# Turned weight products: wide, narrow, narrow, wide in place of wide, narrow, wide, narrow

## The chip, the cores and the metric

The kernel runs on one core of one Trainium2 chip. The metric is the device time of one execution in microseconds (us), as the median of several executions.

## The reference

One decoder block for 256 tokens of 2048 features: a half-step feed-forward, retention and sliding-window heads from one projection, an output projection, cross-attention into 256 memory tokens, a second half-step feed-forward and a last norm. Nearly all of the work is products with weights:

```python
def swiglu(x, w_gate, w_up, w_down):
    return (jax.nn.silu(x @ w_gate) * (x @ w_up)) @ w_down
...
h = h + 0.5 * swiglu(rms_norm(h, ffn1_norm[l]), ffn1_w_gate[l], ffn1_w_up[l], ffn1_w_down[l])
n = rms_norm(h, mix_norm[l])
rq, rk, rv, rg, sq, sk, sv = jnp.split(n @ w_in[l], IN_SPLITS, axis=-1)
...
h = h + jnp.concatenate([ret, swa.astype(h.dtype)], axis=-1) @ w_out[l]
h = h + memory_cross_attention(rms_norm(h, xa_norm[l]), rms_norm(mem, mem_norm[l]), xa_wq[l], xa_wkv[l], xa_wo[l])
h = h + 0.5 * swiglu(rms_norm(h, ffn2_norm[l]), ffn2_w_gate[l], ffn2_w_up[l], ffn2_w_down[l])
return rms_norm(h, final_norm)
```

All of it is float32, with D_MODEL 2048 and D_FF 5632.

## The kernel before

Every float32 factor is used as the exact sum of a high and a low half, `wh` and `wl` for a weight, the two halves of `blk` for an input. ScalarE makes the high half by a copy (`halves`, line 68), VectorE the low half by a subtraction (line 73). A product is high times high plus high times low plus low times high.

The weights come in pieces of 128 x 1024 (tile `wf`, two pieces per DMA, issued by SyncE). One piece is one step of a stream that `run_stream` writes out in program order: at step `at`, `prepare` brings the splitting of pieces up to `at + 3` (LOOKAHEAD), so that `wh` and `wl`, four buffers each, are made some steps ahead. Small tasks (norms, attention) are put between the steps. A group of steps that fill the same accumulator `acc` is a `Unit`; the accumulators have two buffers.

There are two kinds of products. `by_tokens` holds the tokens in the array and calls `three` (lines 361 to 363): three matmuls of 512 columns each. `by_weights`, the turned product that the change touches, holds the weights. A step of it has four tiles `k` of 128 rows and two halves `f` of 128 output features, and for each `(k, f)` it runs two matmuls on the accumulator half `acc[:, f]`:

- a wide one (line 214): the high half of the weights against both halves of the input, 512 columns
- a narrow one (line 215): the low half of the weights against the high half of the input, 256 columns, which is added to the first 256 columns

In the last tile of a unit, the narrow one stands ahead of the wide one (lines 211 and 212). Each matmul has weights of its own, which TensorE loads (LDWEIGHTS, 128 columns) while the matmul ahead of it runs. There are 600 such steps, 4800 wide and 4800 narrow matmuls. A unit over the 2048 features of the model has four steps, 32 wide and 32 narrow ones.

TensorE works its instructions off in the order in which they are written, so the order of the two loops in `by_weights` is the order on the engine.

Of the kernel before, what the change touches and what calls it, by code (L numbers as in the profile page):

```python
# [17 lines left out]
P = 128  # L18
S = 256
# [18 lines left out]
def decoder_block(ctx: ExitStack, tc: tile.TileContext, a: dict, out: bass.AP):  # L38
    nc = tc.nc
# [14 lines left out]
    def blk(dt=F32R):  # L54
        """Four tiles of 128 features by 256 tokens, each as its high and its low half."""
        return work.tile([P, 4, 2, S], dt, tag="blk", name=nm("blk"), bufs=13)
# [13 lines left out]
    def halves(hi, lo, src):  # L70
        """src as the exact sum of two short halves."""
        copy(hi, src)
        nc.vector.tensor_tensor(lo, src, hi, ALU.subtract)  # L73
# [18 lines left out]

    # ------------------------------------------------------------------
    # The stream of weight products, with small tasks between its steps.
    # A product either holds the tokens in the array and gives [tokens, 512 columns], or (turned)
    # holds the weights in it and gives [256 columns, tokens], as two parts still to be added.
    st = {}
    units = []
    tasks = []
# [5 lines left out]
    def when(ready, delay, fn):  # L105
        """fn after a delay, and once ready() holds."""
        def attempt():
            if ready():
                fn()
            else:  # L110
                later(1, attempt)
        later(delay, attempt)
# [16 lines left out]
    class Unit:  # L129
        """One group of n output columns of a product with w, laid out in pieces of 1024 per partition."""  # L130

# [5 lines left out]
        def steps(self):  # L137
            """(unit, block, its tiles of 128 rows, piece of w, first, last)"""
            per = 1024 // self.n
            out = [  # L140
                (self, b, range(i * per, (i + 1) * per), b * (4 // per) + i)
                for b in self.blocks
                for i in range(4 // per)
            ]
            return [x + (i == 0, i == len(out) - 1) for i, x in enumerate(out)]
# [13 lines left out]
    def pin():  # L159
        """Keeps each engine's instructions so far in the order in which they were written."""  # L160
        prev = {}
        for ins in nc.cur_bb.bb.instructions:
            if ins.engine in prev:
                tc.add_manual_dep(
                    ins, prev[ins.engine].name,
                    mybir.DependencyInfo(mybir.DependencyClass.NoSync, mybir.DependencyReason.DATA),
                    reason="program order",
                )
            prev[ins.engine] = ins

    def run_stream():
# [11 lines left out]
        ready = {}  # L183
# [20 lines left out]

        def by_weights(acc, x, wh, wl, first, last):
            for k in range(4):
                for f in range(2):
                    fs = slice(f * P, (f + 1) * P)
                    both, main = acc[:, f, :], acc[:, f, :S]
                    if last and k == 3:  # L210
                        nc.tensor.matmul(main, wl[:, k, fs], x[:, k, 0, :], start=False, stop=False)  # L211
                        nc.tensor.matmul(both, wh[:, k, fs], x[:, k, :, :], start=False, stop=True)  # L212
                    else:
                        nc.tensor.matmul(both, wh[:, k, fs], x[:, k, :, :], start=first and k == 0, stop=False)  # L214
                        nc.tensor.matmul(main, wl[:, k, fs], x[:, k, 0, :], start=False, stop=False)  # L215

# [37 lines left out]

    # ------------------------------------------------------------------
    def turn(src):
        """Transposes src(t, kk) [128 tokens, 128] into two banks of [128, 2, 256]."""
        tp = [tmp_ps() for _ in range(2)]
        for kk in range(4):
            for t in range(2):  # L260
                nc.tensor.transpose(
                    tp[kk // 2][:, (kk % 2) * S + t * P : (kk % 2) * S + (t + 1) * P], src(t, kk), ident
                )
        return tp

    def split_turned(tp, gcol):
        """The exact halves of a turned block, each feature times its gain where there is one."""
        x = blk()
        for b in range(2):
            v = tp[b].rearrange("p (k s) -> p k s", k=2)  # L270
            if gcol is None:
                ks = slice(2 * b, 2 * b + 2)
                halves(x[:, ks, 0, :], x[:, ks, 1, :], v)
            else:
                gained(x[:, 2 * b : 2 * b + 2], v, gcol + 2 * b)
        return x

    def gained(x, v, gcol):
        """x = the exact halves of v, each feature times its gain."""
        for k in range(v.shape[1]):  # L280
            g = gains[:, gcol + k : gcol + k + 1]
            copy(x[:, k, 0, :], v[:, k, :], scale=g)
            nc.vector.scalar_tensor_tensor(x[:, k, 1, :], v[:, k, :], g, x[:, k, 0, :], ALU.mult, ALU.subtract)  # L283

    class Norm:
        """Blocks of a normed and split input [features, tokens], made as the blocks of its source come.

        The blocks lack 1 / rms: the results are multiplied by it, per token."""

# [7 lines left out]
        def block(self, b, src):  # L297
            """src: the block's tiles, [128, n, 256] each."""
            x = blk()
# [6 lines left out]
        def stat(self, src):  # L306
            """Adds the squares of a block to the sums."""
            for v in src:
# [11 lines left out]
        def finish(self):  # L320
            """1 / rms of the tokens, on the partitions."""
            tp = tmp_ps()
# [11 lines left out]
        def spread(self):  # L334
            """The same along the free axis, on every partition."""
            tp = tmp_ps()
# [15 lines left out]
    def total(acc):  # L352
        """The sum of the two parts of a turned product, [128, 2, 256]."""
        x = t2k().rearrange("p (f s) -> p f s", f=2)
# [4 lines left out]
    def three(o, ah, al, bh, bl, start, stop):  # L359
        """o += the product of a sum of halves with another."""  # L360
        nc.tensor.matmul(o, ah, bh, start=start, stop=False)  # L361
        nc.tensor.matmul(o, ah, bl, start=False, stop=False)  # L362
        nc.tensor.matmul(o, al, bh, start=False, stop=stop)  # L363

    # ------------------------------------------------------------------
    def add_to_h(j, acc, factor):
        """Adds 256 features of a turned product to h."""
        v = hT[j // 2][:, 2 * (j % 2) : 2 * (j % 2) + 2, :]
# [5 lines left out]
    def to_h(w, lhs, factor, blocks, norm=None, then=None):  # L374
        """h += factor * (a product with w), and the blocks of the norm that follows."""
        def done(acc, j):
# [47 lines left out]

    # ------------------------------------------------------------------
    n1 = Norm(G_FFN1, "n1")
# [26 lines left out]

    # ------------------------------------------------------------------
    # Retention and sliding-window heads.
    mixT = {}

    def rope(x, t, nh, dst):
        """dst = x [128 tokens, nh, 64] rotated."""
        c, s1, s2 = (  # L460
# [38 lines left out]
    def swa_group(g, t, heads, q, probs):  # L499
        """Scores of some heads for one half of the tokens, and their softmax.  # L500

        The queries' halves lie one above the other and the keys stand twice, so that one pass
        gives (qh + ql) kh and, next to it, (qh + ql) kl."""
        nh = len(heads)
# [196 lines left out]

    # ------------------------------------------------------------------
    # Output projection; the memory's keys and values; cross-attention.
    nxa = Norm(G_XA, "nxa")
# [22 lines left out]
    def put_done(norm, dst, i, f, then=None):  # L727
        """A turned product times 1 / rms, split into its halves, as part of a block."""
        def done(acc):
# [34 lines left out]
    queries = {}  # L764
# [58 lines left out]

    # ------------------------------------------------------------------
    # The last block of products gives [tokens, features]; so does its input then have to be.
    h = []
# [74 lines left out]
def _tables():  # L901
    """Rotary, mask and decay tables: they depend on shapes alone."""
    f = np.float32
# [27 lines left out]
def _pieces(w, n):  # L931
    """w [K, N] as [N / n groups of columns, pieces, 128 rows, 1024]: the pieces in the order in which they are used."""
    k = 1024 // n
# [5 lines left out]
def _turned(x):  # L939
    """x [tokens, features] as [4 blocks * 128 features, 4, tokens]."""  # L940
    return x.T.reshape(4, 4, P, S).transpose(0, 2, 1, 3).reshape(4 * P, 4, S)
# [39 lines left out]
```

## Time and profile before

| | |
|---|---|
| median of 3 runs | 2248.23 us (2248.22 to 2249.44) |
| span of the profiled execution | 2248.1 us |
| PE (matmuls) busy | 2235.6 us, 99% |
| PEld (weight loads) busy | 1932.7 us, 86% |
| DVE (VectorE) busy | 1381.9 us, 61% |
| ACT (ScalarE) busy | 1089.8 us, 48% |
| DMA | 185 GB/s in the mean |

The profiled execution's time is known by its span, 2248.1 us; the timed runs lie 0.1 to 1.3 us above it. The busy time of a matmul in the profile runs to its modelled end and overlaps the next matmul; how long one really takes of the engine is the distance from its start to the start of the next one.

### The profile page before, as it was taken

What the parts mean: (1) busy time and instruction counts of PE and PEld (TensorE: products, weight loads), DVE (VectorE), ACT (ScalarE), POOL (GpSimd) and SP (SyncE); (2) the same over time, 40 slices, a digit from 0 to 9 for tenths busy, and PEclk for the clock granted to TensorE, in tenths of its full rate; (3) what the DMA queues carried; (4) which work ended last, traced back from release to release, by engine and by line L of the source; (5) the groups of instructions that cost most, each with busy time, mean ns of one, the idle gap of its engine ahead of it and who ended that gap; (6) DMA issues with size and microseconds to landing.
All of it is one profiled execution on the core that took longest, in us unless ns stands there. A gap on an engine that the chain in (4) does not pass through costs nothing.

```text
span 2248.1 us, 29814 instructions
## 1 busy us (share of the span) xinstructions
PE 2235.6 (99%) x12310; PEld 1932.7 (86%) x12310; DVE 1381.9 (61%) x1676; ACT 1089.8 (48%) x1371; POOL 13.6 (1%) x17
## 2 busy tenths in 40 slices
PE   9999999999999999999999999999999999999998
PEld 8888888888888888888888888888888888888887
DVE  6656555556566678876765565665656545565554
ACT  5544444444445465545544554555444433444443
POOL 0000000000000000000000000000000000000000
PEclk9999999999999999999999999999999999999999
DMA  7555555555555554445655544455555555555563
GB/s 267 179 185 186 187 186 189 188 187 188 186 197 187 197 169 151 169 167 189 205 186 189 189 167 150 163 185 177 188 187 188 187 188 197 179 187 187 191 216 135
DMA packets 109576, 415.64 MB, mean 185 GB/s; under 512 B 7040, under 2 KB 7040, under 8 KB 109312
## 3 DMA queue, kind: packets, MB, share of 16 engines
q1 hardware_dynamic: 109296, 413.70, 53.8%
q8 instruction: 96, 1.57, 0.3%
q14 instruction: 40, 0.33, 0.0%
q10 hardware_dynamic: 144, 0.05, 0.0%
HBM read 411.62 MB, written 2.10 MB: 184 GB/s over the span
## 4 chain that ended last, share of the span: by engine, by line
PE 98%; DVE 1%; issue 0%; DMA 0%; ACT 0%; SPq 0%; ACTq 0%; POOLq 0%; POOL 0%
PE acc L214 47%; PE acc L215 24%; PE acc L363 7%; PE acc L362 7%; PE acc L361 7%; PE acc L212 3%; PE acc L211 2%; PE tmp L361 0%; PE tmp L363 0%; PE tmp L362 0%; PE tmp L513 0%; DMA wf<-in_ffn_w_gate 0%; PE tmp L539 0%; PE tmp L326 0%; PE tmp L633 0%
## 5 line engine op out<-in xcount | busy, mean ns | idle before, releaser
L214 PE MATMUL acc<-blk,wh 128*128 128x512 f32 x4512 | 1599.3, 398 | 2.8 <-DVE blk L283 2.8
L73 DVE TENSOR_TENSOR wl<-wf,wh 128x1024 fp32r<-128x1024 f32 (+1 forms) x773 | 943.8, 1222 | 621.1 <-ACT wh L68 616.0
L215 PE MATMUL acc<-blk,wl 128*128 128x256 f32 x4512 | 1267.1, 281 | 0.0
L68 ACT ACTIVATE wh<-wf 128x1024 fp32r<-128x1024 f32 (+1 forms) x773 | 816.7, 1057 | 779.1 <-PE acc L214 509.7
L214 PEld LDWEIGHTS acc<-blk,wh 128*128 128x128 f32 x4512 | 848.0, 188 | 201.4 <-DVE blk L283 3.2
L215 PEld LDWEIGHTS acc<-blk,wl 128*128 128x128 f32 x4512 | 853.2, 189 | 6.1 <-DVE wl L73 0.3
L361 PE MATMUL acc<-wh,blk 128*128 128x512 f32 (+1 forms) x704 | 271.6, 386 | 0.0
L362 PE MATMUL acc<-wl,blk 128*128 128x512 f32 (+1 forms) x704 | 270.8, 385 | 0.0
L363 PE MATMUL acc<-wh,blk 128*128 128x512 f32 (+1 forms) x704 | 270.7, 384 | 0.0
L68 ACT ACTIVATE t2k<-acc 128x512 f32<-128x512 f32 x144 | 86.1, 598 | 267.2 <-PE acc L212 265.3
L356 DVE TENSOR_TENSOR t2k<-acc,t2k 128x512 f32<-128x512 f32 x112 | 77.5, 692 | 128.9 <-ACT t2k L68 128.9
L363 PEld LDWEIGHTS acc<-wh,blk 128*128 128x128 f32 x704 | 132.3, 188 | 26.3
L362 PEld LDWEIGHTS acc<-wl,blk 128*128 128x128 f32 x704 | 132.4, 188 | 25.7
L361 PEld LDWEIGHTS acc<-wh,blk 128*128 128x128 f32 x704 | 132.3, 188 | 25.8 <-DVE blk L855 0.2
L212 PE MATMUL acc<-blk,wh 128*128 128x512 f32 x288 | 107.6, 396 | 0.0
L211 PE MATMUL acc<-blk,wl 128*128 128x256 f32 x288 | 81.4, 283 | 0.0
L350 DVE TENSOR_TENSOR t2k<-t2k,rows 128x512 f32<-128x512 f32 x104 | 71.8, 692 | 3.3
L212 PEld LDWEIGHTS acc<-blk,wh 128*128 128x128 f32 x288 | 54.5, 189 | 6.8
L211 PEld LDWEIGHTS acc<-blk,wl 128*128 128x128 f32 x288 | 54.2, 188 | 7.1
L68 ACT ACTIVATE blk<-t2k 128x512 fp32r<-128x512 f32 (+1 forms) x66 | 40.9, 622 | 12.5 <-DVE t2k L350 8.5
L371 DVE TENSOR_TENSOR h<-h,t2k 128x512 f32<-128x512 f32 x32 | 22.2, 692 | 39.2 <-ACT t2k L68 39.2
L73 DVE TENSOR_TENSOR blk<-t2k,blk 128x512 fp32r<-128x512 f32 (+1 forms) x66 | 44.2, 673 | 0.0
(132 smaller groups left out, 691.9 us busy)
## 6 DMA issues: line engine op xcount, KB each, us to landing
wf<-in_ffn_w_gate SPq DMA_DIRECT2D x86, 1024.0 KB, 4.9
wf<-in_ffn_w_up SPq DMA_DIRECT2D x86, 1024.0 KB, 4.9
wf<-in_ffn_w_down SPq DMA_DIRECT2D x84, 1024.0 KB, 4.9
wf<-in_w_in_rqk SPq DMA_DIRECT2D x16, 1024.0 KB, 4.9
wf<-in_w_in_rvg SPq DMA_DIRECT2D x16, 1024.0 KB, 4.8
wf<-in_w_out SPq DMA_DIRECT2D x16, 1024.0 KB, 5.0
wf<-in_xa_wk SPq DMA_DIRECT2D x16, 1024.0 KB, 4.8
wf<-in_xa_wv SPq DMA_DIRECT2D x16, 1024.0 KB, 4.9
```

The source lines that it names most:

```text
L68: return nc.scalar.activation(dst, src, AF.Copy, **kw)
L73: nc.vector.tensor_tensor(lo, src, hi, ALU.subtract)
L211: nc.tensor.matmul(main, wl[:, k, fs], x[:, k, 0, :], start=False, stop=False)
L212: nc.tensor.matmul(both, wh[:, k, fs], x[:, k, :, :], start=False, stop=True)
L214: nc.tensor.matmul(both, wh[:, k, fs], x[:, k, :, :], start=first and k == 0, stop=False)
L215: nc.tensor.matmul(main, wl[:, k, fs], x[:, k, 0, :], start=False, stop=False)
L350: nc.vector.tensor_tensor(x, x, r, ALU.mult)
L356: nc.vector.tensor_tensor(x, acc[:, :, :S], x, ALU.add)
L361: nc.tensor.matmul(o, ah, bh, start=start, stop=False)
L362: nc.tensor.matmul(o, ah, bl, start=False, stop=False)
L363: nc.tensor.matmul(o, al, bh, start=False, stop=stop)
L371: nc.vector.tensor_tensor(v, v, x, ALU.add)
```

## The change

The two matmuls become small functions, and the four of one tile `k` are issued in another order. In the first tile of a unit it is wide, wide, narrow, narrow; in the last one narrow, narrow, wide, wide; in all others wide (f = 0), narrow (f = 0), narrow (f = 1), wide (f = 1). The matmuls themselves, their operands and their number stay as they are.

```diff
         def by_weights(acc, x, wh, wl, first, last):
+            def wide(k, f):
+                nc.tensor.matmul(
+                    acc[:, f, :], wh[:, k, f * P : (f + 1) * P], x[:, k, :, :],
+                    start=first and k == 0, stop=last and k == 3,
+                )
+
+            def narrow(k, f):
+                nc.tensor.matmul(
+                    acc[:, f, :S], wl[:, k, f * P : (f + 1) * P], x[:, k, 0, :], start=False, stop=False
+                )
+
             for k in range(4):
-                for f in range(2):
-                    fs = slice(f * P, (f + 1) * P)
-                    both, main = acc[:, f, :], acc[:, f, :S]
-                    if last and k == 3:
-                        nc.tensor.matmul(main, wl[:, k, fs], x[:, k, 0, :], start=False, stop=False)
-                        nc.tensor.matmul(both, wh[:, k, fs], x[:, k, :, :], start=False, stop=True)
-                    else:
-                        nc.tensor.matmul(both, wh[:, k, fs], x[:, k, :, :], start=first and k == 0, stop=False)
-                        nc.tensor.matmul(main, wl[:, k, fs], x[:, k, 0, :], start=False, stop=False)
+                if first and k == 0:
+                    order = ((wide, 0), (wide, 1), (narrow, 0), (narrow, 1))
+                elif last and k == 3:
+                    order = ((narrow, 0), (narrow, 1), (wide, 0), (wide, 1))
+                else:
+                    order = ((wide, 0), (narrow, 0), (narrow, 1), (wide, 1))
+                for fn, f in order:
+                    fn(k, f)
```

On TensorE, inside a unit: the last two tiles of one step (weights `wh_319`, `wl_320`) and the start of the next (`wh_347`, `wl_348`). Before, lines 214 and 215 are the wide and the narrow matmul:

```order
L214 MATMUL acc_361<-blk_136,wh_319 128x512
L215 MATMUL acc_361<-blk_136,wl_320 128x256
L214 MATMUL acc_361<-blk_136,wh_319 128x512
L215 MATMUL acc_361<-blk_136,wl_320 128x256
L214 MATMUL acc_361<-blk_187,wh_347 128x512
L215 MATMUL acc_361<-blk_187,wl_348 128x256
```

The same place after the change, where line 208 is the wide and line 214 the narrow one, and x2 stands for two in a row:

```order
L208 MATMUL acc_361<-blk_136,wh_319 128x512 x2
L214 MATMUL acc_361<-blk_136,wl_320 128x256 x2
L208 MATMUL acc_361<-blk_136,wh_319 128x512
L208 MATMUL acc_361<-blk_187,wh_347 128x512
L214 MATMUL acc_361<-blk_187,wl_348 128x256 x2
L208 MATMUL acc_361<-blk_187,wh_347 128x512 x2
```

Wide and narrow ones now come in pairs of a kind, across the border of the steps too, and the last matmul of a step is a wide one.

On TensorE, at the border of two units: the last two tiles of accumulator `acc_361` and the first of `acc_467`. Before:

```order
L214 MATMUL acc_361<-blk_285,wh_357 128x512
L215 MATMUL acc_361<-blk_285,wl_358 128x256
L214 MATMUL acc_361<-blk_285,wh_357 128x512
L215 MATMUL acc_361<-blk_285,wl_358 128x256
L211 MATMUL acc_361<-blk_285,wl_358 128x256
L212 MATMUL acc_361<-blk_285,wh_357 128x512
L211 MATMUL acc_361<-blk_285,wl_358 128x256
L212 MATMUL acc_361<-blk_285,wh_357 128x512
L214 MATMUL acc_467<-blk_136,wh_386 128x512
L215 MATMUL acc_467<-blk_136,wl_387 128x256
```

After:

```order
L208 MATMUL acc_361<-blk_285,wh_357 128x512
L214 MATMUL acc_361<-blk_285,wl_358 128x256 x2
L208 MATMUL acc_361<-blk_285,wh_357 128x512 x2
L208 MATMUL acc_467<-blk_136,wh_386 128x512 x2
L214 MATMUL acc_467<-blk_136,wl_387 128x256 x2
L208 MATMUL acc_467<-blk_136,wh_386 128x512
```

Before, the border of two units was the one place with two narrow and two wide ones next to each other; after, four wide ones follow each other there. Over the whole program a narrow one follows a wide one at 4654 places before and at 2400 after; the other engines' instructions stand in the same order, but for a few neighbours.

## Rows read from the trace of the kernel before

**Rows 1.** The page: span, busy time of the engines, granted TensorE clock in 40 slices.

```profile
span 2248.1 us, 29814 instructions
...
PE 2235.6 (99%) x12310; PEld 1932.7 (86%) x12310; DVE 1381.9 (61%) x1676; ACT 1089.8 (48%) x1371; POOL 13.6 (1%) x17
...
PEclk9999999999999999999999999999999999999999
```

**Rows 2.** The page's costliest groups: count, busy us, mean ns, idle before, releaser.

```profile
L214 PE MATMUL acc<-blk,wh 128*128 128x512 f32 x4512 | 1599.3, 398 | 2.8 <-DVE blk L283 2.8
L73 DVE TENSOR_TENSOR wl<-wf,wh 128x1024 fp32r<-128x1024 f32 (+1 forms) x773 | 943.8, 1222 | 621.1 <-ACT wh L68 616.0
...
L68 ACT ACTIVATE wh<-wf 128x1024 fp32r<-128x1024 f32 (+1 forms) x773 | 816.7, 1057 | 779.1 <-PE acc L214 509.7
...
L215 PEld LDWEIGHTS acc<-blk,wl 128*128 128x128 f32 x4512 | 853.2, 189 | 6.1 <-DVE wl L73 0.3
```

**Rows 3.** Groups of matmuls between 100 and 750 us, first feed-forward.

```profile
L214 PE MATMUL acc<-blk,wh 128*128 128x512 f32 x1744 | 616.0, 397 | 0.0
...
L212 PE MATMUL acc<-blk,wh 128*128 128x512 f32 x104 | 38.9, 396 | 0.0
```

**Rows 4.** Timeline, wide matmuls alone (by tokens): start us, us, instruction.

```profile
2174.42 0.39 PE L363 MATMUL acc<-wh,blk 128*128 128x512 f32 x1
...
2176.46 0.39 PE L363 MATMUL acc<-wh,blk 128*128 128x512 f32 x1
```

**Rows 5.** Timeline, narrow matmuls alone (by tokens, the 256-column unit).

```profile
756.51 0.28 PE L361 MATMUL acc<-wh,blk 128*128 128x256 f32 x1
...
757.47 0.28 PE L363 MATMUL acc<-wh,blk 128*128 128x256 f32 x1
```

**Rows 6.** Timeline, a stretch of turned product near 500 us.

```profile
500.06 0.40 PE L214 MATMUL acc<-blk,wh 128*128 128x512 f32 x1
...
500.30 0.28 PE L215 MATMUL acc<-blk,wl 128*128 128x256 f32 x1
...
501.12 0.40 PE L214 MATMUL acc<-blk,wh 128*128 128x512 f32 x1
```

**Rows 7.** Timeline, a stretch of turned product near 310 us.

```profile
309.68 0.39 PE L214 MATMUL acc<-blk,wh 128*128 128x512 f32 x1
309.91 0.28 PE L215 MATMUL acc<-blk,wl 128*128 128x256 f32 x1
...
311.76 0.39 PE L214 MATMUL acc<-blk,wh 128*128 128x512 f32 x1
```

**Rows 8.** Timeline, border of two units at 495 us, and the same place one unit later.

```profile
495.36 0.28 PE L215 MATMUL acc<-blk,wl 128*128 128x256 f32 x1
495.48 0.28 PE L211 MATMUL acc<-blk,wl 128*128 128x256 f32 x1
495.60 0.40 PE L212 MATMUL acc<-blk,wh 128*128 128x512 f32 x1
...
496.19 0.39 PE L214 MATMUL acc<-blk,wh 128*128 128x512 f32 x1
496.41 0.28 PE L215 MATMUL acc<-blk,wl 128*128 128x256 f32 x1
...
506.66 0.28 PE L215 MATMUL acc<-blk,wl 128*128 128x256 f32 x1
```

**Rows 9.** Timeline, border of two units at 299 us.

```profile
298.79 0.28 PE L215 MATMUL acc<-blk,wl 128*128 128x256 f32 x1
...
299.38 0.40 PE L212 MATMUL acc<-blk,wh 128*128 128x512 f32 x1
299.62 0.40 PE L214 MATMUL acc<-blk,wh 128*128 128x512 f32 x1
299.85 0.28 PE L215 MATMUL acc<-blk,wl 128*128 128x256 f32 x1
```

## The prediction

> **What bounds the kernel now.** I read the page first. The matmul engine is busy for 99% of the span of 2248.1 us, and the granted clock is 90% or more of the upper of its two levels, 2.4 GHz, in all 40 slices [rows 1]. The groups of the page say who makes it wait: the wide matmuls waited 2.8 us in all, once, at the start of the program, and the loads of the narrow ones' weights waited 0.3 us for VectorE [rows 2]. ScalarE and VectorE, which feed it, stand idle for about 1.0 us (779.1 over 773) and 0.8 us (621.1 over 773) ahead of each of their pieces, and ScalarE's idle time ends when TensorE gives a weight buffer back [rows 2]. So TensorE sets the pace, and the time is the sum of the distances from the start of one matmul to the start of the next. I therefore read the timeline next, and there starts alone: the column of durations overlaps and says nothing of the pace.
>
> Where only wide matmuls follow each other, nine take 2.04 us, 226.7 ns each [rows 4]. Where only narrow ones follow each other, eight take 0.96 us, 120.0 ns each [rows 5]. One of each at these paces makes 346.7 ns; I call that the pure pace. The alternating stream comes in two forms. Near 310 us six pairs take 2.08 us, 346.7 ns a pair: the pure pace [rows 7]. Near 500 us three pairs take 1.06 us, 353.3 ns a pair [rows 6], 6.7 ns above it, though nothing waits for another engine in either stretch. Which is commoner shows in the count: between 100 and 750 us 1744 + 104 = 1848 wide matmuls of the turned products started [rows 3], 650 us / 1848 = 351.7 ns a pair. That is 5.0 ns above the pure pace, three quarters of 6.7, so about three quarters of the stream runs in the slower form.
>
> **The price of the alternation.** The reader should see that matmuls of one kind keep the pure pace, and that the surplus appears only where kinds alternate. Over 4800 pairs it is 4800 x 5.0 = 24 us, all that an order can give back as long as no matmul runs faster than among its own kind.
>
> The trace also has the new order in small. At each border of two units before the change, two narrow ones follow each other and two wide ones do. The piece from the narrow one at 495.36 to the narrow one at 496.41 holds three of each in 1.05 us; the pure pace would be 1.04, the slower form 1.06 [rows 8]. The same place one unit later is at 506.66: 32 pairs in 11.30 us, where 32 times 353.3 would be 11.307 [rows 8]. So a border, which has one change from wide to narrow and one back fewer than the stream around it, is about 7 ns shorter: the surplus of one pair. Read this way, the surplus belongs to the change of kind, and neighbours of one kind cost nothing.
>
> **The change part by part.**
> - Removed: changes of kind. A narrow one follows a wide one at 4654 places before and 2400 after, by the programs' order. If the surplus goes with these places, at the share of the slower form that the trace has now, it falls from 24 us to 24 x 2400 / 4654 = 12.4 us, a gain of 11.6 us. If every place left pays the whole 6.7 ns, 2400 x 6.7 = 16 us are left and the gain is 8 us. If none does, the gain is 24 us.
> - Added: 2400-odd places where two narrow ones meet and as many where two wide ones do. No stretch of the trace has the four in this order over and over, so their cost is bounded. From below: zero, by rows 4, 5 and 8. From above: the border at 299 us, where the two wide ones that follow each other take 0.47 us (299.38 to 299.85) instead of 0.453, and the piece from 298.79 to 299.85, three of each, takes 1.06 instead of 1.04 [rows 9]. That is 0.02 us on one order of this kind. I take the lower end: the border as in rows 8 is the commoner one by far (92 of the 130 borders that I could follow whole in the timeline took exactly the time of the one in rows 8).
> - Moved: the last use of the high weights goes to the very end of a step, one narrow matmul (0.12 us) later, and that of the low weights to a place one wide matmul earlier. ScalarE waits for that buffer, so it starts 0.12 us later; its 1.0 us of idle time ahead of each piece covers that [rows 2], and pieces are split three steps ahead. Without the cover it would be 0.12 us for each of 600 steps, 72 us. I cost it at nothing. Behind the delayed copy on ScalarE stand the next copies and, on VectorE, the subtraction; both have the idle time named above.
> - In the first tile of a unit the low weights are needed one wide matmul later, in the last tile the accumulator is finished by a wide one as before. Both cost nothing: their waits are 0.3 us in the whole program [rows 2].
> - A faster TensorE takes weights 0.5 to 1% sooner. The feeders' idle time of 0.8 and 1.0 us a piece would shrink by some 0.01 to 0.03 us, for a step of eight pairs is 2.81 us. Nothing there becomes late.
>
> The sum: 2248.1 - 11.6 = 2236.5 us. The timed median lies 0.1 us above the span, which changes nothing.
>
> A rule speaks against all of this. The Trainium skill (TensorE: Matmul & The Clock Gate, Back-to-back issue gap) gives the warm distance as the columns over 2.4 GHz plus about 2.5 ns, 216 and 109 ns, whatever stands beside it; its section on what happens when a matmul is issued adds that loading the next weights takes no read bandwidth from a running matmul. By it order is free and the gain is nothing. The trace does not agree on the size: pure streams take 226.7 and 120.0 ns [rows 4, 5], and alternating ones have two paces at one clock [rows 6, 7].
>
> **The rivals.**
> - The new order runs wholly at the pure pace: the slower form is a rhythm into which the alternation falls (three pairs repeat in 1.06 us), and pairs of a kind break it. For it: 310 us shows a mixed stream without any surplus [rows 7]. Against it: the borders, which break the rhythm, are mostly followed by the slower form again. Time: 2248.1 - 24 = 2224 us.
> - The order is free: the surplus hangs on the mean length of a matmul against its weight load, or on each pair as such, and both orders have as many loads under narrow matmuls, two of four. For it: the two forms in rows 6 and 7 have the same order, so order alone does not fix the pace. Against it: a border saves one surplus [rows 8]. Time: 2248 us, give or take 4. The skill's rule would come out here too.
> - Slower: a change from a pair of a kind to the other kind costs what the border at 299 us shows, 0.02 us, in each group of four, in place of the 2 x 5.0 = 10 ns that a group pays now. For it: such borders exist, and the new order has one such meeting per group. Against it: they are the rarer ones and are followed by a stretch at the pure pace. Price: 2400 groups x (20 - 10) ns = 24 us, 2272 us. It decides from 10 ns a group on; a rhythm of 13 ns a group, 6.7 for each of two changes of kind, would already give 2256.
>
> **How the numbers follow.** The halved surplus, 2236.5 us (2230 to 2243 by its bounds), gets 0.42; the pure pace 0.20; free order 0.20; slower 0.18. A measurement of this kernel can tell about 0.2%, 4.5 us, from no change, so the first two count as faster (0.62), the third as the same, the fourth as slower. For the range I leave out some of the slower case beyond a small surplus and little below the pure pace: 2220 to 2258 us.
>
> **What would show it.** Right: in the timeline a group of wide, narrow, narrow, wide takes 693 to 700 ns from start to start, against 703.4 now (twice 351.7), and its surplus sits where kinds change; the stretch of the first feed-forward shrinks by 0.3 to 1%, while the products by tokens keep their 226.7 ns a matmul. The pure pace as a rival shows 693 everywhere, free order 703, the slower case above it, with the excess where two wide ones meet. Wrong in another way would be new waits of the weight loads on VectorE or of matmuls on ScalarE's copies: then the moved last use costs what I put at nothing. The weakest step is that 32 pairs and one border stand for 2400 groups in an order whose rhythm no row shows.

## The result and the profile after

The change makes the kernel faster: 2235.39 us in the median (2234.9 to 2237.01, 4 runs) against 2248.84 us for the kernel before on the same chip, a ratio of 0.9943 (0.9928 to 0.9957), 13.5 us less. 2236.5 us was forecast.

The page of the changed kernel, span, busy times and the groups that answer to [rows 1, 2]; all wide matmuls are line 208 now, all narrow ones line 214:

```profile
span 2235.2 us, 29666 instructions
...
PE 2222.3 (99%) x12310; PEld 1925.1 (86%) x12310; DVE 1382.0 (62%) x1676; ACT 1088.7 (49%) x1371; POOL 9.4 (0%) x17
...
L208 PE MATMUL acc<-blk,wh 128*128 128x512 f32 x4800 | 1518.0, 396 | 3.4 <-DVE blk L294 3.4
L73 DVE TENSOR_TENSOR wl<-wf,wh 128x1024 fp32r<-128x1024 f32 (+1 forms) x773 | 944.0, 1222 | 628.5 <-ACT wh L68 622.8
L68 ACT ACTIVATE wh<-wf 128x1024 fp32r<-128x1024 f32 (+1 forms) x773 | 817.0, 1058 | 791.0 <-PE acc L208 516.0
L214 PEld LDWEIGHTS acc<-blk,wl 128*128 128x128 f32 x4800 | 903.5, 188 | 199.0
...
L208 PEld LDWEIGHTS acc<-blk,wh 128*128 128x128 f32 x4800 | 756.6, 189 | 16.3 <-DVE blk L294 3.8
```

TensorE still sets the pace at 99%, and still waits 3.4 us once, at the start. The feeders take as long as before and stand idle a little more ahead of the weight pieces (ScalarE 791 us against 779, VectorE 629 against 621). No load waits for VectorE's low halves: no cost of giving a weight buffer back one narrow matmul later can be seen.

The same stretch as [rows 3], 100 to 750 us:

```profile
L208 PE MATMUL acc<-blk,wh 128*128 128x512 f32 x1863 | 585.0, 395 | 0.0
L214 PE MATMUL acc<-blk,wl 128*128 128x256 f32 x1866 | 368.0, 279 | 0.0
```

1863 wide ones in 650 us are 348.9 ns for a wide and a narrow one, against 351.7. If all 4800 pairs gain as these do, the difference of 2.8 ns is 13.4 us, the whole gain. The surplus over the pure pace of 346.7 ns fell from 5.0 to 2.2 ns a pair, from 24 to 11 us.

In the timeline of the changed kernel, neighbours of a kind stand merged into one line, and the first column gives each run's start:

```profile
499.13 0.63 PE L208 MATMUL acc<-blk,wh 128*128 128x512 f32 x2
499.60 0.39 PE L214 MATMUL acc<-blk,wl 128*128 128x256 f32 x2
499.83 0.63 PE L208 MATMUL acc<-blk,wh 128*128 128x512 f32 x2
500.29 0.40 PE L214 MATMUL acc<-blk,wl 128*128 128x256 f32 x2
500.52 0.63 PE L208 MATMUL acc<-blk,wh 128*128 128x512 f32 x2
...
501.92 0.63 PE L208 MATMUL acc<-blk,wh 128*128 128x512 f32 x2
```

From 499.13 to 501.92 four groups take 2.79 us, 697 ns each: within the 693 to 700 that I gave as the sign of a right forecast. But look where the surplus sits. Two narrow ones take 0.23 us (0.24 at the pure pace), two wide ones 0.46 to 0.47 (0.453). The wide ones are slow, the narrow ones are quick; it is not that neighbours of a kind keep the pure pace. The trace of the whole run shows a steady rhythm here: of the 1761 groups of wide, wide, narrow, narrow that two more wide ones follow, 1602 take 694 to 698 ns, most of them by turns with distances of about 233, 236, 116, 112 and 233, 231, 113, 119. The kernel before had another one: at 3978 places three pairs follow each other, and at 3090 of them they took 1060 ns, the slower form, at 526 1040, the pure pace.

### The profile page after: what moved, and what is told of

Its sections match the earlier page's. It is cut to its first block, busy times and chain, and to the rows that moved or that the text cites. A ratio compares the mean times of both kernels' runs of the same rounds, so it can differ in the third digit from the quotient of the medians.

```text
span 2235.2 us, 29666 instructions
## 1 busy us (share of the span) xinstructions
PE 2222.3 (99%) x12310; PEld 1925.1 (86%) x12310; DVE 1382.0 (62%) x1676; ACT 1088.7 (49%) x1371; POOL 9.4 (0%) x17
## 4 chain that ended last, share of the span: by engine, by line
PE 98%; DVE 1%; issue 0%; DMA 0%; ACT 0%; SPq 0%; ACTq 0%; POOLq 0%; POOL 0%
PE acc L208 50%; PE acc L214 25%; PE acc L374 7%; PE acc L372 7%; PE acc L373 7%; PE tmp L372 0%; PE tmp L374 0%; PE tmp L373 0%; DMA wf<-in_ffn_w_gate 0%; PE tmp L524 0%; PE tmp L550 0%; PE tmp L337 0%; PE tmp L644 0%; DVE wl L73 0%; PE tmp L848 0%
## 5 line engine op out<-in xcount | busy, mean ns | idle before, releaser
L208 PE MATMUL acc<-blk,wh 128*128 128x512 f32 x4800 | 1518.0, 396 | 3.4 <-DVE blk L294 3.4
L214 PE MATMUL acc<-blk,wl 128*128 128x256 f32 x4800 | 948.5, 279 | 0.0
L208 PEld LDWEIGHTS acc<-blk,wh 128*128 128x128 f32 x4800 | 756.6, 189 | 16.3 <-DVE blk L294 3.8
L408 ACT ACTIVATE t2k<-t2k 128x512 f32<-128x512 f32 x44 | 27.8, 632 | 22.6 <-DVE t2k L361 22.6
L68 ACT ACTIVATE blk<-tmp 128x512 fp32r<-128x512 f32 (+3 forms) x57 | 25.8, 469 | 23.1 <-DVE blk L73 14.0
L68 ACT ACTIVATE blk<-h,gains 128x256 fp32r<-128x256 f32 x64 | 28.4, 500 | 8.1 <-DVE h L383 7.9
L419 DVE TENSOR_TENSOR t2k<-t2k,t2k 128x512 f32<-128x512 f32 x44 | 30.1, 686 | 0.0
```

The lines of the kernel that those rows point to most:

```text
L68: return nc.scalar.activation(dst, src, AF.Copy, **kw)
L208: nc.tensor.matmul(acc[:, f, :], wh[:, k, f * P : (f + 1) * P], x[:, k, :, :], start=first and k == 0, stop=last and k == 3,)
L214: nc.tensor.matmul(acc[:, f, :S], wl[:, k, f * P : (f + 1) * P], x[:, k, 0, :], start=False, stop=False)
L408: nc.scalar.activation(s, s, AF.Silu)
L419: nc.vector.tensor_tensor(s, s, gated.pop((b, f)), ALU.mult)
```

## The experiments

All runs are compared with the kernel before on the same chip. A place is a narrow matmul that follows a wide one: 4654 before, 2400 in the change. The diffs are cut to the lines that matter; unless the text says otherwise, they start from the changed kernel.

**Fewest places: runs of eight.**

```diff
-            for k in range(4):
-                ...
+            wides = [(wide, k, f) for k in range(4) for f in range(2)]
+            narrows = [(narrow, k, f) for k in range(4) for f in range(2)]
+            for fn, k, f in narrows + wides if last else wides + narrows:
+                fn(k, f)
```

> All eight wide matmuls of a step first, then its eight narrow ones (in a unit's last step the narrow ones first). A narrow one follows a wide one at 460 places, against 4654 before and 2400 in the change. Theory 1, a price for each change of kind: the change took 13 us for 2254 places, 6.0 ns a place, so 4194 places fewer give 25 us, about 2223 us. Theory 2, the rhythm of the repeated pattern sets the surplus, not the count of places: any value from 2224 to 2248, by the rhythm that runs of eight fall into. Theory 3, the price sits where a narrow one follows a wide one into the same half of the accumulator: no such place is left, 2224 us.

2233.18 us, 0.9927 (0.9914 to 0.9941). With 460 places it gains 16 us, not 25. Theories 1 and 3 fall. The timeline shows the cost of a run:

```profile
500.12 3.82 PE L208 MATMUL acc<-blk,wh 128*128 128x512 f32 x16
503.77 1.11 PE L214 MATMUL acc<-blk,wl 128*128 128x256 f32 x8
504.72 2.00 PE L208 MATMUL acc<-blk,wh 128*128 128x512 f32 x8
506.56 1.12 PE L214 MATMUL acc<-blk,wl 128*128 128x256 f32 x8
507.52 0.86 PE L208 MATMUL acc<-blk,wh 128*128 128x512 f32 x3
```

Eight wide ones take 1.84 us (504.72 to 506.56) where the pure pace gives 1.813, sixteen take 3.65 (500.12 to 503.77) where it gives 3.627: some 25 ns more in both, whatever their number. Eight narrow ones take 0.95 to 0.96, the pure 0.96 or a little less. One by one, the wide ones behind narrow ones are 233, 236, 228, 233, 231 ns apart and 226 to 227 from then on; the narrow ones behind wide ones 113, 119 and 120 from then on. So a return to wide ones costs 27 ns, spread over five of them, and a step to narrow ones gives 7 back: 20 ns net. I call this passage the transient.

**Runs of two that never meet in one half of the accumulator.**

```diff
-                    order = ((wide, 0), (narrow, 0), (narrow, 1), (wide, 1))
+                    order = ((wide, 0), (wide, 1), (narrow, 0), (narrow, 1))
```

> Wide, wide, narrow, narrow in every group (narrow, narrow, wide, wide in a unit's last one). A narrow one follows a wide one at 2254 places, about as many as in the change, but always into the other half of the accumulator. Theory 1, a price for each change of kind: 2248.2 - 6.0 ns x 2400 = 2234 us, the time of the change. Theory 2, the rhythm: a pattern of its own within a unit is the same as that of the change, runs of two, so the time is that of the change but for the borders, 2232 to 2240 us. Theory 3, the same half: no such place is left, 2224 us.

2233.96 us, 0.9933 (0.9921 to 0.9946): the time of the change within the interval. Which half of the accumulator the neighbours write plays no part that these runs can tell.

**The border alone, and the middle alone.** The first keeps the order of before in the middle of a unit and takes the change's first and last group; the second does it the other way round.

```diff
-                    order = ((wide, 0), (narrow, 0), (narrow, 1), (wide, 1))
+                    order = ((wide, 0), (narrow, 0), (wide, 1), (narrow, 1))
```

> The order of before in the middle of a unit, that of the change in its first and last group alone. A narrow one follows a wide one at 4366 places. Theory 1, a price for each change of kind: 288 places fewer, 1.7 us, 2246.5 us. Theory 2, the rhythm: the borders decide whether the faster or the slower form of the alternation follows, so 2230 (the faster form in most units) or 2248 (the slower one), and not in proportion to the places. Theory 3, the same half: as theory 1, 2246 us.

2250.93 us, 1.0007 (0.9998 to 1.0015): no gain, though it has 288 places fewer. From 100 to 750 us it started 1844 wide ones, hardly fewer than the 1848 of before:

```profile
L208 PE MATMUL acc<-blk,wh 128*128 128x512 f32 x1844 | 636.8, 398 | 0.0
```

```diff
-                    order = ((wide, 0), (wide, 1), (narrow, 0), (narrow, 1))
+                    order = ((wide, 0), (narrow, 0), (wide, 1), (narrow, 1))
...
-                    order = ((narrow, 0), (narrow, 1), (wide, 0), (wide, 1))
+                    order = ((narrow, 0), (wide, 0), (narrow, 1), (wide, 1))
```

> The order of the change in the middle of a unit, that of before in its first and last group. A narrow one follows a wide one at 2688 places. Theory 1, a price for each change of kind: 288 places more than the change, 1.7 us, 2237 us. Theory 2, the rhythm: the groups behind a border took 705 to 709 ns in the trace of the change, those in the middle of a unit 697; if the border of the change upsets the rhythm, the border of before gives 1 to 3 us back, 2232 to 2234 us. Theory 3, the same half: 2237 us.

2236.08 us, 0.9942 (0.9929 to 0.9954): the whole gain. The border's new order neither helps nor hurts.

**Four by four.** As in the run of eights, but each half of a step (two of its four tiles) by itself.

```diff
+            for half in range(2):
+                wides = [(wide, 2 * half + k, f) for k in range(2) for f in range(2)]
+                narrows = [(narrow, 2 * half + k, f) for k in range(2) for f in range(2)]
+                for fn, k, f in narrows + wides if last and half == 1 else wides + narrows:
+                    fn(k, f)
```

> Four wide ones, four narrow ones, by turns; a narrow one follows a wide one at 1055 places. In the run of eights each return to wide ones cost 27 ns, spread over the first five of them (233, 236, 228, 233, 231 instead of 226.7), and each step to narrow ones gave 7 ns back. Theory 4, this transient: four wide ones take 930 ns instead of 906.7, four narrow ones 472 instead of 480, 15 ns for four pairs, 1200 times: 18 us of surplus beside some 2.5 us elsewhere, 20 us against 28.6 us before: 2240 us. Theory 1, 6.0 ns for each change of kind: 2248.2 - 6.0 ns x 3600 = 2227 us. Between the measured eights and twos (a smooth optimum): 2233 us.

2240.97 us, 0.9962 (0.9948 to 0.9975): slower than runs of two and runs of eight both (its ratio's interval touches that of the change, but its fastest run, 2239.73, is above the change's slowest, 2237.01), as the transient of theory 4 has it (2240), and against any price for each place (2227). Its timeline:

```profile
510.44 0.63 PE L214 MATMUL acc<-blk,wl 128*128 128x256 f32 x4
510.92 1.09 PE L208 MATMUL acc<-blk,wh 128*128 128x512 f32 x4
511.84 0.64 PE L214 MATMUL acc<-blk,wl 128*128 128x256 f32 x4
512.32 1.09 PE L208 MATMUL acc<-blk,wh 128*128 128x512 f32 x4
513.25 0.63 PE L214 MATMUL acc<-blk,wl 128*128 128x256 f32 x4
```

Four wide ones take 0.92 to 0.93 us where the pure pace gives 0.907: they pay most of the 27 ns, and about twice as often as in runs of eight.

**Sixteen by sixteen.** Every second step turns its two runs round, so that runs meet across steps. The diff starts from the run of eights.

```diff
+            turned_last[0] = last or not (first or turned_last[0])
-            for fn, k, f in narrows + wides if last else wides + narrows:
+            for fn, k, f in narrows + wides if turned_last[0] else wides + narrows:
```

> Eight wide and eight narrow ones in one step, eight narrow and eight wide ones in the next, so that kinds change every sixteen matmuls; a narrow one follows a wide one at 308 places. Theory 4, the transient: 20 ns at each of 308 places, 6.2 us, beside 2.5 us elsewhere, 8.7 us of surplus against 11.7 us in the run of eights: 3 us less than that, 2230 us. If the rest of the surplus has nothing to do with the changes of kind, it stays at 2233 us. Theory 1: 2222 us.

2229.96 us, 0.9914 (0.9900 to 0.9927), as the transient has it, and the fastest of all: 19 us under the kernel before, and 5 us below the changed one, whose interval it just does not overlap.

```profile
503.57 3.82 PE L210 MATMUL acc<-blk,wh 128*128 128x512 f32 x16
507.23 2.08 PE L216 MATMUL acc<-blk,wl 128*128 128x256 f32 x16
509.14 3.14 PE L210 MATMUL acc<-blk,wh 128*128 128x512 f32 x13
```

Sixteen wide ones take 3.66 us (pure 3.627), sixteen narrow ones 1.91 (pure 1.92).

**Is the load under a narrow matmul the cause?** Two runs keep the order of before and give each narrow matmul more columns, so that it lasts longer than a weight load. The diff is that for 384 columns, without the loop, which goes back to the order of before; the other run has 288.

```diff
-                    acc[:, f, :S], wl[:, k, f * P : (f + 1) * P], x[:, k, 0, :], start=False, stop=False
+                    acc[:, f, :384], wl[:, k, f * P : (f + 1) * P],
+                    x[:, k, :, :].rearrange("p c s -> p (c s)")[:, :384], start=False, stop=False,
```

> The order of before, but each narrow matmul has 288 columns in place of 256 (it adds low times low for 32 tokens, which the kernel before leaves out). 288 columns at 2.4 GHz are 120 ns, more than the 112 ns that weight loads alone take from start to start in the trace; 256 columns are 106.7 ns, less. Theory 5, the surplus is there because a narrow matmul is shorter than the next load, and each matmul costs 13.3 ns beside its columns: no surplus is left, 346.7 + 13.3 = 360 ns a pair, 2248 - 29 + 64 = 2284 us. Theory 5b, the same but the pace is columns times 17/16 (226.7 and 113.3) and 120 ns is the load's: 354 ns a pair, 2256 us. Theory 6, the surplus belongs to the alternation of widths as such: 2312 us.

2304.92 us, 1.0246 (1.0232 to 1.0260): between theories 5 and 6. From 100 to 750 us:

```profile
L208 PE MATMUL acc<-blk,wh 128*128 128x512 f32 x1789 | 645.1, 395 | 0.0
```

650 us / 1789 = 363.3 ns a pair. If 288 columns take columns plus 13.3 ns among themselves, which no run shows, the pure pace is 360: the surplus shrinks from 5.0 to 3.3 ns and does not vanish.

> The order of before, but each narrow matmul has 384 columns in place of 256 (it adds low times low for 128 tokens, which the kernel before leaves out): 160 ns of columns, well above the load's 112 ns. Theory 5, a matmul shorter than the next load, with 13.3 ns beside the columns: 346.7 + 53.3 = 400 ns a pair, 2248 - 29 + 256 = 2475 us. Theory 5b, columns times 17/16: 396.7 ns a pair, 2460 us. Theory 6, the alternation as such, 6.7 ns a pair: 2504 us.

2540.95 us, 1.1297 (1.1282 to 1.1313): above all three forecasts, the nearest of them theory 6. In its timeline five pairs take 2.06 us, 412 ns each:

```profile
499.94 0.40 PE L208 MATMUL acc<-blk,wh 128*128 128x512 f32 x1
...
502.00 0.40 PE L208 MATMUL acc<-blk,wh 128*128 128x512 f32 x1
```

What 384 columns take among themselves was missing, so the run of eights was repeated with the same diff.

> Eight wide and eight narrow ones by turns as in the run of eights, but each narrow one has 384 columns in place of 256 (it adds low times low for 128 tokens). It gives the pace of 384 columns among themselves, which the alternating run with 384 columns lacks. If that pace is columns plus 13.3 ns, 173.3 ns, and the return to wide ones costs the same 20 ns net: 2233 + 4800 x 53.3 ns = 2489 us. If the transient comes only behind matmuls that are shorter than a weight load: no transient, 2480 us. If the 180 ns of the alternating run are the pace of 384 columns themselves: 2521 us.

2509.6 us, 1.1159 (1.1143 to 1.1176). One by one, the last ones of a run of 384 columns are 173 to 174 ns apart, columns plus 13.3 ns as at 256 and 512. The pure pace of a pair is thus 400 ns, and the alternation with 384 columns pays 12 to 13 ns above it, twice what it pays with 256. The timeline of the eights:

```profile
509.30 2.01 PE L208 MATMUL acc<-blk,wh 128*128 128x512 f32 x8
511.15 1.58 PE L214 MATMUL acc<-blk,wl 128*128 128x384 f32 x8
512.57 2.01 PE L208 MATMUL acc<-blk,wh 128*128 128x512 f32 x8
514.42 2.96 PE L214 MATMUL acc<-blk,wl 128*128 128x384 f32 x16
```

Eight wide ones take 1.85 us (pure 1.813), eight of 384 columns 1.42 (pure 1.387): here both steps cost, some 35 ns each, which the 2489 us expected had left out. The transient is longer too: one by one, it takes nine wide ones or six of 384 columns to come back to the pure pace. So the cost does not need a matmul that is shorter than the next load. That it comes from the change of width, and not from the change of operands that goes with it, fits the products by tokens: they alternate between high and low halves at one width and keep 226.7 ns [rows 4].

**The alternation without any border.** The last matmul of a unit is a narrow one, so that wide and narrow follow each other through all units. The diff starts from the kernel before.

```diff
-                    if last and k == 3:
-                        nc.tensor.matmul(main, wl[:, k, fs], x[:, k, 0, :], start=False, stop=False)
-                        nc.tensor.matmul(both, wh[:, k, fs], x[:, k, :, :], start=False, stop=True)
-                    else:
-                        ...
+                    nc.tensor.matmul(
+                        acc[:, f, :], wh[:, k, f * P : (f + 1) * P], x[:, k, :, :], start=first and k == 0, stop=False
+                    )
+                    nc.tensor.matmul(
+                        acc[:, f, :S], wl[:, k, f * P : (f + 1) * P], x[:, k, 0, :], start=False, stop=last and k == 3
+                    )
```

> Wide, narrow, wide, narrow without a break, over the borders of units too (the last matmul of a unit is a narrow one). A narrow one follows a wide one at 4793 places. If the alternation as such falls into the slower form and the borders only now and then push it into the faster one: 6.7 ns for each pair, 32 us of surplus against 28.6 us before, 2252 us. If the borders keep it from the faster form: 346.7 ns a pair, 2221 us. Theory 4, the transient cut short after one matmul (233 + 113 ns a pair): the same, 2221 us.

Neither: ten runs of this one program lie in two groups, six from 2232.48 to 2237.42 us and four from 2247.19 to 2251.41, at nearly the same granted clock (0.998 to 0.999 and 0.997 to 0.999). The ratio of 0.9967 (0.9946 to 0.9988) is a mean over both. The profiled execution, one of the first group, has both forms in it. From 100 to 700 us:

```profile
L220 PE MATMUL acc<-blk,wh 128*128 128x512 f32 x1732 | 600.5, 391 | 0.0
...
```

and from 1600 to 1750 us:

```profile
L220 PE MATMUL acc<-blk,wh 128*128 128x512 f32 x426 | 150.6, 399 | 0.0
...
```

600 us / 1732 = 346.4 ns, the pure pace, for the whole first stretch; 150 us / 426 = 352.1 in the second. The order is the same in both. Once in a form, the unbroken alternation stays in it for hundreds of microseconds.

## Why the prediction was right in the time and wrong in a step

- **TensorE's sequence of starts is the time:** right. The gain of the first feed-forward, scaled to 4800 pairs, is 13.4 us, nearly the whole difference of 13.5.
- **The pure pace is the floor, and 24 us are all that an order can give back:** it held. No order came below 2229.96 us by its median, and the wide and narrow ones keep columns plus 13.3 ns in long runs; the stretch of 600 us at 346.4 ns shows that a mixed order can reach it.
- **The failed step** is this: "Read this way, the surplus belongs to the change of kind, and neighbours of one kind cost nothing." Halving the number of places halved the surplus (24 to 11 us, 12.4 forecast), but not because each place has a price. With a fifth of the change's places the run of eights has hardly less of it (2 us by the medians), and with half of them the run of fours has more. That 11.6 us of forecast gain met 13.5 is luck: the same price for each place missed the run of eights by 10 us and that of fours by 14. What the runs show in its place: the distance from one matmul to the next depends on several matmuls ahead of it, not on its neighbour alone. Behind a change of width (256 and 512 columns) it runs off the pure pace and comes back within about five wide ones. A run of eight or sixteen pays the whole of it once (20 ns net), a run of four most of it, about twice as often. With that, the runs of four and of sixteen were forecast within 1 us (2240 and 2230; 2240.97 and 2229.96 measured).
- **Runs of two** escape about half of it: 697 ns a group, some 4 ns above the pure pace of 693, where the first two distances of the transient (233 + 236 + 113 + 119) would give 701. The transient does not begin afresh at each change, so it does not tell what short runs do; their rhythm has to be measured. Theory 2, that the repeated pattern sets the surplus, is what is left for them: of the first three theories it alone allowed both for wide, wide, narrow, narrow at the time of the change and for a border without effect, and the trace shows the rhythm itself (697 and 696 ns by turns). But it left the run of eights open (2224 to 2248), and its guess that the border of before gives 1 to 3 us back missed (2236.08).
- **The border as a model of the new order** [rows 8, 9] gave the right size for a wrong reason: the border alone is worth nothing (1.0007), the middle alone is worth everything (0.9942). The bounds put beside the 2236.5 us, 2230 to 2243, do not come out of the prediction's own list either: gains of 8 to 24 us give 2224 to 2240.
- **The moved last use at no cost, and feeders with room to spare:** right, as the page after shows. The idle time ahead of the weight pieces did not shrink, as forecast, but grew by 12 us on ScalarE and 7 us on VectorE.
- **The rivals.** Free order falls: eight other orders of the same matmuls gave medians from 2230 to 2251 us. The Trainium skill's formula (TensorE: Matmul & The Clock Gate, Back-to-back issue gap) of columns over 2.4 GHz plus 2.5 ns has the right shape, but the constant is 13.3 ns here at three widths, and what follows a change of width is missing from it. That section gives it for the isolated distance, not for a stream with a weight load ahead of each matmul, so "whatever stands beside it" was more than the Trainium skill says. The pure pace everywhere was not reached by the change, though the borderless run shows that it exists. The slower case did not come: two wide ones do take 0.47 us as at 299 us [rows 9], but the narrow ones beside them are quicker in return.

What stays open is the mechanism behind the transient and the rhythms. The load under a short matmul is excluded as the sole cause by the runs with 384 columns, and the half of the accumulator, as far as these runs can tell, by the order wide, wide, narrow, narrow. That the weight loads and the moving columns disturb each other fits a cost that depends on how their phases fall, and two stable forms of one order; no run here takes the loads away, so it is argued and not shown.

## What to carry to other kernels

Where TensorE is busy for 99%, read the distances from start to start, not the durations: they show a few per cent between the columns' time and what a matmul takes. Group matmuls of one width into long runs (here sixteen, 0.9914), or try short patterns and measure; do not count changes of kind, for runs of four were worse than runs of two. And when one order shows two paces at one clock in one trace, expect that its time may differ between executions, as it did for the borderless one (the kernel before, which also shows both paces, stayed within 3.3 us), and prefer an order whose runs are long enough to come back to the pure pace.

## What the runs showed of the hardware

One program, the alternation without borders, differs by 19 us between executions (2232.48 to 2251.41) with nearly the same clock. Its one trace holds both forms of the stream; that the share of each sets the time of an execution is inferred from that. The kernel before does not show that (2247.53 to 2250.82 over 13 runs).

The start varies too. Granted clock (the column behind the busy times of the five engines, as a share of 2.4 GHz) in four stretches of the changed kernel's profile; the first busy time is TensorE's:

```profile
6.00:9.00 3.00, 0.29 (x3) 0.10 (x1) 0.47 (x1) 1.14 (x3) 0.00 (x0) 0.99 1.00 367
9.00:12.00 3.00, 2.33 (x8) 2.04 (x9) 2.73 (x6) 2.31 (x5) 0.00 (x0) 0.50 1.03 419
12.00:15.00 3.00, 3.00 (x11) 2.52 (x11) 2.48 (x5) 3.00 (x6) 0.00 (x0) 0.50 1.03 419
15.00:18.00 3.00, 3.00 (x17) 2.59 (x16) 3.00 (x5) 2.68 (x6) 0.00 (x0) 0.87 1.06 407
```

and in the run of sixteens, whose instructions up to there are of the same kind:

```profile
6.00:9.00 3.00, 1.18 (x5) 0.85 (x5) 1.47 (x4) 2.13 (x5) 0.00 (x0) 1.00 0.98 381
9.00:12.00 3.00, 3.00 (x18) 2.63 (x17) 2.03 (x4) 1.91 (x3) 0.00 (x0) 1.00 1.03 421
```

In the first, TensorE was busy for 0.29 of the 3 us ahead of 9 us, and the clock is at the lower level (1.2 GHz) from there until after 15 us; in the second it was busy for 1.18 us, and the clock stays at 2.4 GHz. Between 9 and 15 us the rows of the first count 19 matmuls; the second has 18 by 12 us. These are two kernels with one profile each, but the kernel before alone had mean granted clocks from 0.997 (2249.96 to 2250.82 us) to 0.999 (2247.53 to 2249.60 us) in its executions. So some 3 us of the difference between two spans need have nothing to do with the order, and I took the gain of the change from the stretch after 100 us.
